# Attention and mLSTM outputs: the 64-row products grouped by bank, and the mLSTM's output gate emptied by VectorE before its sigmoids

## The chip, the cores and the metric

One core of a Trainium2 chip runs the kernel. The metric is device time in microseconds (us) from start to end, median of three runs. TensorE (PE in the profile) multiplies, VectorE (DVE), ScalarE (ACT) and GpSimd (POOL) work element by element, and SyncE (SP) issues most transfers. A matmul contracts over the rows (partitions) of its operands: up to 128 of them, here 128 or 64. It writes to a bank of PSUM, up to 512 f32 values in every partition here; the kernel has four banks (`mm`) for the large products and four (`ax`) for the small ones.

## The reference, cut to what matters

One decoder layer over 512 tokens and 1024 channels, in f32. Its mixer runs three branches on the same normalised input. Two of them carry a matrix state for each of four heads, with keys of 64 and values of 128 channels:

```python
# gated linear attention, chunk by chunk
o_inter = einsum('bhld,bhdv->bhlv', qi * exp(cum), state)
o = o_inter + einsum('bhij,bhjv->bhiv', scores, vi)

# mLSTM, chunk by chunk
scores = einsum('bhtd,bhsd->bhts', qi, ki) * exp(d_intra - m_t[..., None])
num = w_inter[..., None] * einsum('bhtd,bhdv->bhtv', qi, mem) + einsum('bhts,bhsv->bhtv', scores, vi)
den = w_inter * einsum('bhtd,bhd->bht', qi, norm) + scores.sum(-1)
h = num / maximum(abs(den), exp(-m_t))[..., None]
y_ml = sigmoid(mo) * h          # mo: a projection of the layer's input
```

The third branch is a state-space layer (S5) with a gelu. The branches are projected, weighted by sigmoid gates, summed and projected by `w_out`; a SwiGLU network of two large products follows.

## The kernel before, in words

The kernel takes chunks of 128 tokens, four of them (`t` = 0 to 3). A head's state has 64 rows, one for each key channel, so two heads lie in one tile: head `h = 2p + hh` has the rows `64 hh` to `64 hh + 63` of pair `p`. The output of a chunk adds two products for each head: the scores with the values (`ST` with `gv` in attention, L1169; `Sc` with `mvp` in the mLSTM, L1459), which contract over the 128 tokens of the chunk, and the scaled queries with the state before the chunk (`qE` with `Sg`, L1173; `qw` with `mem`, L1462), which contract over 64 rows. Chunk 0 has no state before it, so only the first. Two `ax` banks take a chunk, one for each `hh`; a bank holds the heads of both pairs side by side. mLSTM columns are 129, the last one for the denominator.

Attention's banks are emptied by VectorE into `og` (L226, four operations a chunk); ScalarE squares them, VectorE makes the norm and multiplies by the gate `gr`, and PE transposes the result (L1196 in `to_fm`). The mLSTM's banks go through ScalarE (absolute value) and VectorE (reciprocal, then `ym`, which multiplies by the gate `mo`), and are transposed in the same function. In `scores(t)`, PE multiplies keys and queries over 64 rows (L1448) and VectorE multiplies by the decay `Wd`.

Between such steps the large projections run: `fill(n)` takes the next pieces of a list of jobs (`gv`, `su`, `gr`, merge gates, `mx`, `mo`, `mv`, `glu`, ...). Each weight block comes by a transfer of SP (L319), is split into a high part `hi` by ScalarE and a rest `lo` by VectorE (both f32r), and is multiplied in three passes of 512 columns (L422 to L424, and L454 to L456 where tokens are the output's rows). `mo` is such a job: four banks, one for each chunk, emptied by `ev_mo` (L645). The next job, `mv`, needs the same four banks.

The program gives an order, but the framework schedules the mixer again, engine by engine, from its own estimates; only the head of the kernel and everything from the output projection on keep a written order. So an edit in the mixer may also move instructions that it does not name. The S5 branch runs among the `mo` products: its state products (L1314 and L1315) read `U`, `M`, `Xs` and `CA`; `Xs` comes from VectorE's scan, rotations and products, and `M` from SP's loads of `kd_d` (L1269). `conv` are the mLSTM's four tiles of queries and keys, made of four VectorE steps each and a silu; `Y` is the gelu of the S5 output, `rho` an activation of its decay, `WT` the copied states. Different functions of ScalarE need different tables, loaded by ACT_TABLE_LOAD.

Of the kernel before, what the change touches and what calls it, by code (L numbers as in the profile page):

```python
# [8 lines left out]
AF = mybir.ActivationFunctionType  # L9
OP = mybir.AluOpType  # L10
# [166 lines left out]
def _body(tc, A, out):  # L177
    nc = tc.nc
    act, dve, pool, pe, sp = nc.scalar, nc.vector, nc.gpsimd, nc.tensor, nc.sync
    from contextlib import ExitStack  # L180
    with ExitStack() as ctx:
        _emit(tc, nc, ctx, ExitStack, A, out, act, dve, pool, pe, sp)


def _emit(tc, nc, ctx, ExitStack, A, out, act, dve, pool, pe, sp):
# [23 lines left out]
    def slot(name="s", dt=F32, tag="s"):  # L209
        return pools[tag].tile([128, 512], dt, tag=tag, name=name)  # L210
# [4 lines left out]
    def ax_bank(name="ax"):  # L215
        return axp.tile([128, 512], F32, tag="ax", name=name)


    def tt(e, o, a, b, op):
        e.tensor_tensor(out=o, in0=a, in1=b, op=op)  # L220
# [4 lines left out]
    def stt(o, a, s, b, op0, op1):  # L225
        dve.scalar_tensor_tensor(out=o, in0=a, scalar=s, in1=b, op0=op0, op1=op1)  # L226

    def af(o, i, f, **kw):
        act.activation(out=o, in_=i, func=f, **kw)  # L229

    def cp(o, i, e=dve):
        e.tensor_copy(out=o, in_=i)
# [6 lines left out]
    mm = pe.matmul  # L239
# [69 lines left out]
    class Stream:  # L309
        loaded = done = 0  # L310
        raw, hl = {}, {}
        start = None
# [178 lines left out]
    i = 0  # L491
# [21 lines left out]
    ST = {}  # L513
# [46 lines left out]
    w, h, u, r = (st[:, 4 * i:4 * i + 4] for i in range(4))  # L560
# [9 lines left out]
    for t in range(4):  # L570
        tk = slice(t * 128, (t + 1) * 128)
# [51 lines left out]
    gv, gr, mo = {}, {}, {}  # L623
    conv = {}
# [19 lines left out]

    def ev_mo(t, ps):  # L645
        mo[t] = slot("mo", tag="v")
        af(mo[t], ps, AF.Sigmoid)

    def ev_conv(f):
        def e(ps):  # L650
# [163 lines left out]
    for f in range(4):  # L814
        job(f"mx{f}", fm_job(A["wmx"], f, ev_conv(f)))
    job("mo", tm_job(A["wmo"], ev_mo))
    job("mv", tm_job(A["wmv"], ev_mv), lambda: "v" in ML)
    glu_idx = [add_item(A["wgl"][j // 2][:, (j % 2) * 512:(j % 2 + 1) * 512], w=512) for j in range(4)]
# [111 lines left out]
    for p in range(2):  # L930
        ps = ax_bank()
# [149 lines left out]
    qk, qE, ecum, kdT, Sg = {}, {}, {}, {}, {}  # L1081
# [39 lines left out]
    for p in range(2):  # L1121
        qk[p] = slot("qk")
        tt(dve, qk[p], qT[p], kT[p], OP.mult)
        for t in range(4):
            mm(dps[:, t * 4 + p * 2:t * 4 + p * 2 + 2], lhsT=qk[p][:, t * 128:(t + 1) * 128], rhs=C("heads"),
               start=True, stop=True)
    cp(dg, dps[:, 0:16])
    for p in range(2):
# [10 lines left out]
        ps = ax_bank()  # L1139
# [6 lines left out]
    for p in range(2):  # L1146
        Sg[p] = slot("Sg", tag="y")
        for t in range(3):
            ps = ax_bank()
            mm(ps[:, 0:256], lhsT=kdT[p][:, t * 128:(t + 1) * 128], rhs=gv[t][:, p * 256:(p + 1) * 256],  # L1150
               start=True, stop=True)
            for h in range(2):
                r = slice(64 * h, 64 * h + 64)
                o = Sg[p][r, t * 128:(t + 1) * 128]
# [7 lines left out]
    ssg, rg = st3[:, 16:32], st3[:, 32:48]  # L1162
    for t in range(4):
        ps = [ax_bank(), ax_bank()]
        for h in range(4):
            p, hh = h // 2, h % 2
            o = ps[hh][:, p * 128:(p + 1) * 128]
            a = (t % 2) * 2 + hh
            mm(o, lhsT=ST[p, t // 2][:, a * 128:(a + 1) * 128], rhs=gv[t][:, h * 128:(h + 1) * 128],  # L1169
               start=True, stop=(t == 0))  # L1170
            if t > 0:
                r = slice(64 * hh, 64 * hh + 64)
                mm(o, lhsT=qE[p][r, t * 128:(t + 1) * 128], rhs=Sg[p][r, (t - 1) * 128:t * 128],  # L1173
                   start=False, stop=True)
        og[t] = slot("og")
        for h in range(4):
            sl = slice(h * 128, (h + 1) * 128)
            stt(og[t][:, sl], gv[t][:, sl], dg[:, t * 4 + h:t * 4 + h + 1],
                ps[h % 2][:, (h // 2) * 128:(h // 2 + 1) * 128], OP.mult, OP.add)
            junk = slot("junk")  # L1180
            af(junk[:, 0:128], og[t][:, sl], AF.Square, accum_out=ssg[:, t * 4 + h:t * 4 + h + 1])
        fill(1)
# [162 lines left out]
    mvp = vp.tile([128, 4, 4, 129], F32, name="mvp")  # L1345
# [3 lines left out]
    def mslot(name="m"):  # L1349
        return mp.tile([128, 512], F32, tag="m", name=name)  # L1350
# [36 lines left out]
    ps = ax_bank()  # L1387
# [6 lines left out]
    wI, qw, kw, mem = {}, {}, {}, {}  # L1394
    for p in range(2):
        ps = ax_bank()
# [3 lines left out]
    Wd = {}  # L1400
# [11 lines left out]
    for p in range(2):  # L1412
        qw[p] = mslot("qw")
        stt(qw[p], conv[p], 0.125, wI[p], OP.mult, OP.mult)
        ps = ax_bank()
# [8 lines left out]
    for p in range(2):  # L1424
        mem[p] = mslot("mem")
        for t in range(3):
            ps = ax_bank()
            mm(ps[:, 0:258], lhsT=kw[p][:, t * 128:(t + 1) * 128],
               rhs=mvp[:, t, 2 * p:2 * p + 2].rearrange("p h v -> p (h v)"), start=True, stop=True)
            for h in range(2):  # L1430
                r = slice(64 * h, 64 * h + 64)
                o = mem[p][r, t * 129:(t + 1) * 129]
# [6 lines left out]
    ym, Sc = {}, {}  # L1439

    def scores(t):
        tk = slice(t * 128, (t + 1) * 128)
        Sc[t] = mslot("Sc")
        for hh in range(2):
            ps = ax_bank()
            r = slice(64 * hh, 64 * hh + 64)
            for p in range(2):
                mm(ps[:, p * 128:(p + 1) * 128], lhsT=conv[2 + p][r, tk], rhs=conv[p][r, tk], start=True, stop=True)  # L1448
            v = lambda a: a.rearrange("p (q h i) -> p q h i", q=2, h=2)[:, :, hh]
            stt(v(Sc[t]), ps[:, 0:256].rearrange("p (q i) -> p q i", q=2), 0.125, v(Wd[t]), OP.mult, OP.mult)  # L1450

    def heads_out(t):
        ym[t] = slot("ym")
        for hh in range(2):
            ps = ax_bank()
            for p in range(2):
                o = ps[:, p * 129:(p + 1) * 129]
                h = 2 * p + hh
                mm(o, lhsT=Sc[t][:, h * 128:(h + 1) * 128], rhs=mvp[:, t, h], start=True, stop=(t == 0))  # L1459
                if t > 0:  # L1460
                    r = slice(64 * hh, 64 * hh + 64)
                    mm(o, lhsT=qw[p][r, t * 128:(t + 1) * 128], rhs=mem[p][r, (t - 1) * 129:t * 129],  # L1462
                       start=False, stop=True)
            den = st3[:, 32 + 4 * (t % 2) + 2 * hh:34 + 4 * (t % 2) + 2 * hh]
            pv_ = ps[:, 0:258].rearrange("p (q v) -> p q v", q=2)
            ac = st3[:, 48 + 4 * (t % 2) + 2 * hh:50 + 4 * (t % 2) + 2 * hh]
            af(ac.unsqueeze(2), pv_[:, :, 128:129], AF.Abs)
            ev = em.rearrange("p (t q h) -> p t q h", q=2, h=2)[:, t, :, hh]
            tt(dve, den, ac, ev, OP.max)
            dve.reciprocal(out=den, in_=den)  # L1470
            for p in range(2):
                h = 2 * p + hh
                sl = slice(h * 128, (h + 1) * 128)
                stt(ym[t][:, sl], ps[:, p * 129:p * 129 + 128], den[:, p:p + 1], mo[t][:, sl], OP.mult, OP.mult)

    scores(0)
    for t in range(4):
        if t < 3:
            decay(t + 1)
            fill(1)  # L1480
            scores(t + 1)
        heads_out(t)
        fill(1)
# [255 lines left out]
```

## Time and profile before

| | |
|---|---|
| runs | 917.51, 920.76, 921.31 us; median 920.76 |
| profiled execution | 917.74 us, of which the span is 915.9 |
| PE busy | 896.3 us, 98% |
| DVE busy | 574.0 us, 63% |
| ACT busy | 332.7 us, 36%; 31 table loads of 1283 ns among them |
| PE's granted clock | 9 tenths or more in all but the first of 40 slices |
| transfers | 120.79 MB, mean 132 GB/s |

The view that carries most is the timeline of an engine: start, busy time, line, output and inputs, shape, how many in a row, and in brackets the idle time before and what ended it. On PE an f32 product is two passes, which the timeline counts as x2; the f32r products of 512 columns are one each. Matmuls are pipelined, so the next one starts before the time of the one before has run out: what a piece of work costs is seen in the distance between starts.

### The profile page before, as it was taken

What the parts mean: (1) busy time and instruction counts of PE and PEld (TensorE: products, weight loads), DVE (VectorE), ACT (ScalarE), POOL (GpSimd) and SP (SyncE); (2) the same over time, 40 slices, a digit from 0 to 9 for tenths busy, and PEclk for the clock granted to TensorE, in tenths of its full rate; (3) what the DMA queues carried; (4) which work ended last, traced back from release to release, by engine and by line L of the source; (5) the groups of instructions that cost most, each with busy time, mean ns of one, the idle gap of its engine ahead of it and who ended that gap; (6) DMA issues with size and microseconds to landing.
All of it is one profiled execution on the core that took longest, in us unless ns stands there. A gap on an engine that the chain in (4) does not pass through costs nothing.

```text
span 915.9 us, 11578 instructions
## 1 busy us (share of the span) xinstructions
PE 896.3 (98%) x4334; PEld 726.7 (79%) x4334; DVE 574.0 (63%) x1140; ACT 332.7 (36%) x513; POOL 24.9 (3%) x68
## 2 busy tenths in 40 slices
PE   8999999999989999999999989999999999999997
PEld 7668887778878878778888867888888888888885
DVE  6848999879879974965669487634444333322215
ACT  4339323431442481622334454422332223211113
POOL 1010000000000000000010000000000000000000
PEclk8999999999999999999999999999999999999999
DMA  9661431234542442434455543533333333322304
GB/s 363 247 192 47 127 116 58 68 122 120 158 141 103 120 115 92 137 106 161 155 183 203 188 163 116 177 121 132 116 114 123 118 105 114 115 92 93 115 1 137
DMA packets 52193, 120.79 MB, mean 132 GB/s; under 512 B 13797, under 2 KB 19429, under 8 KB 52137
## 3 DMA queue, kind: packets, MB, share of 16 engines
q1 hardware_dynamic: 49944, 115.92, 37.9%
q0 software_dynamic: 1040, 2.38, 1.1%
q10 hardware_dynamic: 1152, 1.75, 0.5%
q8 instruction: 34, 0.56, 0.2%
q14 instruction: 23, 0.18, 0.1%
HBM read 113.21 MB, written 6.82 MB: 131 GB/s over the span
## 4 chain that ended last, share of the span: by engine, by line
PE 80%; DVE 15%; issue 2%; ACT 2%; DMA 1%; SPq 0%; DVEq 0%; ACTq 0%
PE mm L422 16%; PE mm L424 16%; PE mm L423 16%; PE y L1519 5%; PE y L1520 5%; PE y L1521 5%; DVE lo L220 2%; PE mm L455 2%; PE mm L454 2%; PE mm L456 2%; DVE ST L1108 1%; DVE Qp L220 1%; DVE D L220 1%; PE ax L1314 1%; PE ax L1315 1%
## 5 line engine op out<-in xcount | busy, mean ns | idle before, releaser
L229 ACT ACTIVATE hi<-raw 128x1024 fp32r<-128x1024 f32 (+2 forms) x157 | 151.9, 971 | 389.4 <-PE mm L423 161.4
L220 DVE TENSOR_TENSOR lo<-raw,hi 128x1024 fp32r<-128x1024 f32 (+2 forms) x157 | 174.6, 1114 | 152.3 <-ACT hi L229 151.6
L424 PE MATMUL mm<-h2hi,lo 128*128 128x512 f32 x320 | 124.6, 389 | 0.0
L423 PE MATMUL mm<-h2lo,hi 128*128 128x512 f32 x320 | 124.6, 389 | 0.0
L422 PE MATMUL mm<-h2hi,hi 128*128 128x512 f32 x320 | 124.5, 389 | 0.0
L424 PE MATMUL mm<-hT,lo 128*128 128x512 f32 x280 | 110.9, 396 | 3.1 <-DVE lo L220 3.1
L422 PE MATMUL mm<-hT,hi 128*128 128x512 f32 x280 | 112.3, 401 | 1.2 <-ACT hT L229 1.2
L423 PE MATMUL mm<-hT,hi 128*128 128x512 f32 x280 | 110.9, 396 | 0.5 <-DVE hT L226 0.4
L423 PEld LDWEIGHTS mm<-h2lo,hi 128*128 128x128 f32 x320 | 60.1, 188 | 12.6
L422 PEld LDWEIGHTS mm<-h2hi,hi 128*128 128x128 f32 x320 | 60.1, 188 | 12.5
L424 PEld LDWEIGHTS mm<-h2hi,lo 128*128 128x128 f32 x320 | 60.1, 188 | 12.3
L1521 PE MATMUL y<-hi,g 128*128 128x512 f32 x176 | 68.5, 389 | 0.0
L1520 PE MATMUL y<-lo,g 128*128 128x512 f32 x176 | 68.5, 389 | 0.0
L1519 PE MATMUL y<-hi,g 128*128 128x512 f32 x176 | 68.3, 389 | 0.0
L422 PEld LDWEIGHTS mm<-hT,hi 128*128 128x128 f32 x280 | 53.0, 189 | 16.8 <-issue 4.4
L220 DVE TENSOR_TENSOR sg<-sg,mm 128x512 f32<-128x512 f32 x36 | 24.7, 685 | 65.8 <-PE mm L424 65.8
L424 PEld LDWEIGHTS mm<-hT,lo 128*128 128x128 f32 x280 | 53.1, 190 | 14.9 <-DVE lo L220 3.5
L423 PEld LDWEIGHTS mm<-hT,hi 128*128 128x128 f32 x280 | 53.1, 190 | 11.9 <-DVE hT L226 1.3
L226 DVE SCALAR_TENSOR_TENSOR gacc<-raw,cact,gacc 128x512 f32<-128x512 f32 x56 | 41.9, 748 | 21.7 <-DMA raw<-ada 21.1
L455 PE MATMUL mm<-lo,hT 128*128 128x512 f32 x128 | 50.5, 395 | 0.4 <-DVE lo L220 0.4
L454 PE MATMUL mm<-hi,hT 128*128 128x512 f32 x128 | 49.8, 399 | 0.0
L456 PE MATMUL mm<-hi,hT 128*128 128x512 f32 x128 | 49.7, 391 | 0.0
(310 smaller groups left out, 1404.4 us busy)
## 6 DMA issues: line engine op xcount, KB each, us to landing
raw<-ada SPq DMA_DIRECT2D x48, 512.0 KB, 3.6
raw<-ffn SPq DMA_DIRECT2D x44, 512.0 KB, 3.4
raw<-wzg SPq DMA_DIRECT2D x24, 512.0 KB, 3.3
raw<-ffo SPq DMA_DIRECT2D x22, 512.0 KB, 3.3
raw<-wpr SPq DMA_DIRECT2D x24, 256.0 KB, 2.7
raw<-wout SPq DMA_DIRECT2D x8, 512.0 KB, 3.3
raw<-sweep SPq DMA_DIRECT2D x8, 384.0 KB, 9.0
xT<-xT SPq DMA_DIRECT2D x4, 512.0 KB, 5.6
```

The costliest lines, as they stand in the source:

```text
L220: e.tensor_tensor(out=o, in0=a, in1=b, op=op)
L226: dve.scalar_tensor_tensor(out=o, in0=a, scalar=s, in1=b, op0=op0, op1=op1)
L229: act.activation(out=o, in_=i, func=f, **kw)
L422: mm(ps, lhsT=whi, rhs=xhi, start=first, stop=False)
L423: mm(ps, lhsT=whi, rhs=xlo, start=False, stop=False)
L424: mm(ps, lhsT=wlo, rhs=xhi, start=False, stop=last)
L454: mm(ps[t], lhsT=xh[:, tk], rhs=hi[:, sl], start=(k == 0), stop=False)
L455: mm(ps[t], lhsT=xh[:, tk], rhs=lo[:, sl], start=False, stop=False)
L456: mm(ps[t], lhsT=xl[:, tk], rhs=hi[:, sl], start=False, stop=(k == 7))
L1519: mm(ps, lhsT=xhi, rhs=whi[:, sl], start=first, stop=False)
L1520: mm(ps, lhsT=xhi, rhs=wlo[:, sl], start=False, stop=False)
L1521: mm(ps, lhsT=xlo, rhs=whi[:, sl], start=False, stop=last)
```

## The change

In attention's output and in the mLSTM's (`heads_out`) the loop over heads becomes two: first the four 64-row products of a chunk, then the four 128-row products on top of them. In `scores` all four products are issued ahead of VectorE's two steps, with both banks taken first. In `ev_mo` VectorE copies each bank out of PSUM, and after the fourth copy ScalarE does the four sigmoids in place.

```diff
     def ev_mo(t, ps):
         mo[t] = slot("mo", tag="v")
-        af(mo[t], ps, AF.Sigmoid)
+        cp(mo[t], ps)
+        if t == 3:
+            for u in range(4):
+                af(mo[u], mo[u], AF.Sigmoid)
...
         ps = [ax_bank(), ax_bank()]
+
+        for h in range(4 if t else 0):
+            p, hh = h // 2, h % 2
+            r = slice(64 * hh, 64 * hh + 64)
+            mm(ps[hh][:, p * 128:(p + 1) * 128], lhsT=qE[p][r, t * 128:(t + 1) * 128],
+               rhs=Sg[p][r, (t - 1) * 128:t * 128], start=(p == 0), stop=False)
         for h in range(4):
             p, hh = h // 2, h % 2
-            o = ps[hh][:, p * 128:(p + 1) * 128]
             a = (t % 2) * 2 + hh
-            mm(o, lhsT=ST[p, t // 2][:, a * 128:(a + 1) * 128], rhs=gv[t][:, h * 128:(h + 1) * 128],
-               start=True, stop=(t == 0))
-            if t > 0:
-                r = slice(64 * hh, 64 * hh + 64)
-                mm(o, lhsT=qE[p][r, t * 128:(t + 1) * 128], rhs=Sg[p][r, (t - 1) * 128:t * 128],
-                   start=False, stop=True)
+            mm(ps[hh][:, p * 128:(p + 1) * 128], lhsT=ST[p, t // 2][:, a * 128:(a + 1) * 128],
+               rhs=gv[t][:, h * 128:(h + 1) * 128], start=(t == 0 and p == 0), stop=(p == 1))
...
         Sc[t] = mslot("Sc")
+        ps = [ax_bank(), ax_bank()]
+        for p in range(2):
+            for hh in range(2):
+                r = slice(64 * hh, 64 * hh + 64)
+                mm(ps[hh][:, p * 128:(p + 1) * 128], lhsT=conv[2 + p][r, tk], rhs=conv[p][r, tk], start=True, stop=True)
         for hh in range(2):
-            ps = ax_bank()
-            r = slice(64 * hh, 64 * hh + 64)
-            for p in range(2):
-                mm(ps[:, p * 128:(p + 1) * 128], lhsT=conv[2 + p][r, tk], rhs=conv[p][r, tk], start=True, stop=True)
...
         ym[t] = slot("ym")
+        pss = [ax_bank(), ax_bank()]
+        for h in range(4 if t else 0):
+            p, hh = h // 2, h % 2
+            r = slice(64 * hh, 64 * hh + 64)
+            mm(pss[hh][:, p * 129:(p + 1) * 129], lhsT=qw[p][r, t * 128:(t + 1) * 128],
+               rhs=mem[p][r, (t - 1) * 129:t * 129], start=(p == 0), stop=False)
+        for h in range(4):
+            p, hh = h // 2, h % 2
+            mm(pss[hh][:, p * 129:(p + 1) * 129], lhsT=Sc[t][:, h * 128:(h + 1) * 128], rhs=mvp[:, t, h],
+               start=(t == 0 and p == 0), stop=(p == 1))
         for hh in range(2):
-            ps = ax_bank()
-            for p in range(2):
-                o = ps[:, p * 129:(p + 1) * 129]
-                h = 2 * p + hh
-                mm(o, lhsT=Sc[t][:, h * 128:(h + 1) * 128], rhs=mvp[:, t, h], start=True, stop=(t == 0))
-                if t > 0:
-                    r = slice(64 * hh, 64 * hh + 64)
-                    mm(o, lhsT=qw[p][r, t * 128:(t + 1) * 128], rhs=mem[p][r, (t - 1) * 129:t * 129],
-                       start=False, stop=True)
+            ps = pss[hh]
```

The scheduler decides where these instructions come to stand. On PE, attention's chunk 1 before (`ax_1587` and `ax_1588` are its two banks, for the row halves A, rows 0 to 63, and B, 64 to 127; the numbers are those of buffers):

```order
L1169 MATMUL ax_1587<-gv_959,ST_118 128x128
L1173 MATMUL ax_1587<-Sg_1481,qE_1429 128x128
L1169 MATMUL ax_1587<-gv_959,ST_122 128x128
L1173 MATMUL ax_1587<-Sg_1512,qE_1443 128x128
L1169 MATMUL ax_1588<-gv_959,ST_118 128x128
L1173 MATMUL ax_1588<-Sg_1481,qE_1429 128x128
L1169 MATMUL ax_1588<-gv_959,ST_122 128x128
L1173 MATMUL ax_1588<-Sg_1512,qE_1443 128x128
```

After:

```order
L1172 MATMUL ax_1587<-Sg_1481,qE_1429 128x128
L1172 MATMUL ax_1587<-Sg_1512,qE_1443 128x128
L1177 MATMUL ax_1587<-gv_959,ST_118 128x128
L1177 MATMUL ax_1587<-gv_959,ST_122 128x128
L1172 MATMUL ax_1588<-Sg_1481,qE_1429 128x128
L1172 MATMUL ax_1588<-Sg_1512,qE_1443 128x128
L1177 MATMUL ax_1588<-gv_959,ST_118 128x128
L1177 MATMUL ax_1588<-gv_959,ST_122 128x128
```

The banks stay apart, and in each the two 64-row products stand before the two 128-row products. The mLSTM's chunk 1 has the same form.

On PE, the mLSTM's chunk 2 before (banks `ax_3683` and `ax_3693`; chunk 3 follows at once in the same form):

```order
L1459 MATMUL ax_3683<-mvp_3097,Sc_3601 128x129
L1462 MATMUL ax_3683<-mem_3439,qw_3402 128x129
L1459 MATMUL ax_3683<-mvp_3097,Sc_3601 128x129
L1462 MATMUL ax_3683<-mem_3473,qw_3410 128x129
L1459 MATMUL ax_3693<-mvp_3097,Sc_3601 128x129
L1462 MATMUL ax_3693<-mem_3439,qw_3402 128x129
L1459 MATMUL ax_3693<-mvp_3097,Sc_3601 128x129
L1462 MATMUL ax_3693<-mem_3473,qw_3410 128x129
```

After (banks `ax_3687` and `ax_3688`):

```order
L1463 MATMUL ax_3687<-mem_3443,qw_3406 128x129
L1463 MATMUL ax_3687<-mem_3477,qw_3414 128x129
L1463 MATMUL ax_3688<-mem_3443,qw_3406 128x129
L1463 MATMUL ax_3688<-mem_3477,qw_3414 128x129
L1467 MATMUL ax_3687<-mvp_3097,Sc_3605 128x129
L1467 MATMUL ax_3688<-mvp_3097,Sc_3605 128x129
L1467 MATMUL ax_3687<-mvp_3097,Sc_3605 128x129
L1467 MATMUL ax_3688<-mvp_3097,Sc_3605 128x129
```

Four 64-row products, the half A twice and the half B twice, then four 128-row products. Chunk 3 follows at once in the same form; so do attention's chunks 2 (A, A, B, B) and 3 (A, B, A, B), each by itself.

On ACT, a piece of the difference at the place where the `mo` products begin (`hi_2956` is the high part of the second weight block of `mo`; `Y_2849` and `rho_2943` belong to the S5 branch):

```order
-L229 ACTIVATE hi_2956<-raw_2799 128x1024
 L229 ACTIVATE WT_2773<-ax_2774 128x512
 L229 ACTIVATE WT_2773<-ax_2780 128x512
 L229 ACT_TABLE_LOAD
+L229 ACTIVATE conv_2826<-conv_2826 128x512
+L229 ACT_TABLE_LOAD
 L229 ACTIVATE Y_2849<-ax_2832 128x512
 L229 ACTIVATE rho_2943<-w5_732 128x256 x2
 L229 ACT_TABLE_LOAD
-L229 ACTIVATE conv_2826<-conv_2826 128x512
 L229 ACTIVATE conv_2883<-conv_2883 128x512
+L229 ACTIVATE hi_2956<-raw_2799 128x1024
```

One silu of `conv` with a table load of its own has moved ahead of the gelu, and `hi_2956` from ahead of `WT` to behind the second silu. Further on the four sigmoids of `mo` stand in a row where they were two pairs, with the two exponentials `wI` ahead of them. On DVE the four copies of `mo` stand ahead of `Wd` of chunk 0. On SP one load of the weights of `mv` has moved behind eight loads of `M`.

## Rows read from the trace of the kernel before

**Rows 1.** Page, busy us (share of the span) and instructions of an engine.

```profile
PE 896.3 (98%) x4334; PEld 726.7 (79%) x4334; DVE 574.0 (63%) x1140; ACT 332.7 (36%) x513; POOL 24.9 (3%) x68
```

**Rows 2.** Waits of PE, 175 to 425 us: total, times, longest.

```profile
PE mm L424 <- DVE lo L220: 3.1, 1, 3.1
PE ax L1196 <- DVE og L226: 0.7, 1, 0.7
```

**Rows 3.** Timeline of PE, 151 us: start, busy time, line, out<-in, shape, count.

```profile
151.11 0.61 PE L1169 MATMUL ax<-gv,ST 128*128 128x128 f32 x4
...
151.79 0.39 PE L424 MATMUL mm<-hT,lo 128*128 128x512 f32 x1
```

**Rows 4.** Timeline of PE, 369 to 376 us: 64-row products of the scores.

```profile
369.14 0.40 PE L424 MATMUL mm<-hi,lo 128*128 128x512 f32 x1
369.47 0.72 PE L1448 MATMUL ax<-conv 64*128 64x128 f32 x8
...
370.46 0.40 PE L422 MATMUL mm<-yhi,hi 128*128 128x512 f32 x1
...
373.88 0.39 PE L422 MATMUL mm<-hT,hi 128*128 128x512 f32 x1
374.20 0.71 PE L1448 MATMUL ax<-conv 64*128 64x128 f32 x4
...
375.18 0.39 PE L424 MATMUL mm<-hT,lo 128*128 128x512 f32 x1
```

**Rows 5.** Timeline of PE, attention's chunk 2.

```profile
158.54 0.39 PE L424 MATMUL mm<-hT,lo 128*128 128x512 f32 x1
158.77 0.38 PE L1169 MATMUL ax<-gv,ST 128*128 128x128 f32 x2
159.08 0.48 PE L1173 MATMUL ax<-Sg,qE 64*128 64x128 f32 x2
...
162.34 0.39 PE L423 MATMUL mm<-hT,hi 128*128 128x512 f32 x1
```

**Rows 6.** Timeline of DVE, attention's outputs of chunks 2 and 3.

```profile
163.43 1.11 DVE L226 SCALAR_TENSOR_TENSOR og<-gv,st,ax 128x128 f32<-128x128 f32 x4
167.36 0.61 DVE L226 SCALAR_TENSOR_TENSOR og<-gv,st,ax 128x128 f32<-128x128 f32 x2 [2.81 <-PE ax L1173]
168.19 0.60 DVE L226 SCALAR_TENSOR_TENSOR og<-gv,st,ax 128x128 f32<-128x128 f32 x2 [0.23 <-PE ax L1173]
```

**Rows 7.** Timeline of PE at three places.

```profile
314.32 0.33 PE L1315 MATMUL ax<-Xs,CA 128*128 128x64 f32 x2
...
333.51 0.48 PE L454 MATMUL mm<-hi,hT 128*128 128x512 f32 x1
...
411.83 1.25 PE L1196 MATMUL ax<-ident,ym 128*128 128x128 f32 x10
```

**Rows 8.** Timeline of DVE at three places.

```profile
311.45 1.71 DVE L220 TENSOR_TENSOR Xs<-x,y 64x252 f32<-64x252 f32 x4
...
337.88 1.23 DVE L220 TENSOR_TENSOR lo<-raw,hi 128x1024 fp32r<-128x1024 f32 x1 [1.54 <-ACT hi L229]
...
407.64 1.13 DVE L226 SCALAR_TENSOR_TENSOR ym<-ax,st,mo 128x128 f32<-128x128 f32 x4
```

**Rows 9.** Timeline of ACT, 294 to 331 us.

```profile
294.67 1.06 ACT L229 ACTIVATE hi<-raw 128x1024 fp32r<-128x1024 f32 x1 [5.17 <-PE mm L423]
...
297.60 1.28 ACT L229 ACT_TABLE_LOAD   x1
...
303.22 1.29 ACT L229 ACTIVATE conv<-conv 128x512 f32<-128x512 f32 x2 [0.92 <-DVE conv L226]
...
330.50 1.08 ACT L229 ACTIVATE mo<-mm 128x512 f32<-128x512 f32 x2
```

**Rows 10.** Costliest groups: copies of mv (busy us, mean ns, idle before).

```profile
L232 DVE COPY mvp<-mm 128x512 f32<-128x512 f32 x4 | 2.7, 692 | 2.0 <-PE mm L456 2.0
```

**Rows 11.** SP's queue, loads of M.

```profile
306.14 3.62 SPq L1269 DMA_DIRECT2D M<-kd_d  x8
```

More of the change, by code (lines that the diff above doesn't have):

```diff
@@ L1443, in scores @@
         Sc[t] = mslot("Sc")
+        ps = [ax_bank(), ax_bank()]
[3 more added lines that the diff above has]
+                mm(ps[hh][:, p * 128:(p + 1) * 128], lhsT=conv[2 + p][r, tk], rhs=conv[p][r, tk], start=True, stop=True)
         for hh in range(2):
-            ps = ax_bank()
-            r = slice(64 * hh, 64 * hh + 64)
-            for p in range(2):
-                mm(ps[:, p * 128:(p + 1) * 128], lhsT=conv[2 + p][r, tk], rhs=conv[p][r, tk], start=True, stop=True)
             v = lambda a: a.rearrange("p (q h i) -> p q h i", q=2, h=2)[:, :, hh]
-            stt(v(Sc[t]), ps[:, 0:256].rearrange("p (q i) -> p q i", q=2), 0.125, v(Wd[t]), OP.mult, OP.mult)
+            stt(v(Sc[t]), ps[hh][:, 0:256].rearrange("p (q i) -> p q i", q=2), 0.125, v(Wd[t]), OP.mult, OP.mult)
     def heads_out(t):
         ym[t] = slot("ym")
-        for hh in range(2):
-            ps = ax_bank()
-            for p in range(2):
-                o = ps[:, p * 129:(p + 1) * 129]
-                h = 2 * p + hh
-                mm(o, lhsT=Sc[t][:, h * 128:(h + 1) * 128], rhs=mvp[:, t, h], start=True, stop=(t == 0))
-                if t > 0:
-                    r = slice(64 * hh, 64 * hh + 64)
-                    mm(o, lhsT=qw[p][r, t * 128:(t + 1) * 128], rhs=mem[p][r, (t - 1) * 129:t * 129],
-                       start=False, stop=True)
+        pss = [ax_bank(), ax_bank()]
[8 more added lines that the diff above has]
+               start=(t == 0 and p == 0), stop=(p == 1))
+        for hh in range(2):
+            ps = pss[hh]
             den = st3[:, 32 + 4 * (t % 2) + 2 * hh:34 + 4 * (t % 2) + 2 * hh]
```

## The prediction

> **What bounds the kernel.** I read the busy table first: TensorE (PE) is busy 98% of the span [rows 1]. Then PE's waits from the attention outputs (175 us) to the end of the mLSTM (425): two rows, 3.1 and 0.7 us [rows 2]. So a microsecond taken out of PE's own row of work reaches the end, unless another engine has to come earlier too; each saving below is followed to where PE next waits. The profiled execution took 917.74 us around a span of 915.9; the sum is made against 917.74. The median shown, 920.76, is 3.02 us (0.33%) above it, and the result is scaled by 920.76/917.74. Half a per cent, about what a measurement of this kernel can tell from no change, is 4.6 us.
>
> **Price of a switch between 128-row and 64-row products.** Each f32 product stands as two passes (x2 in the rows), and 512-column matmuls start 0.23 us apart. A block is charged from the start that the next matmul would have had without it to the start of the second matmul behind it, less one spacing. Four 128-row passes between 512-column matmuls: 151.11 to 151.79 less 0.23, 0.45 us, or 0.115 a pass with no switch [rows 3]. Four 64-row passes of one row half: 373.88 to 375.18 less two spacings, 0.85; less 4 x 0.115 that leaves 0.39 for two switches, 0.19 each [rows 4]. One attention chunk with its alternating products: 158.54 to 162.34 less two spacings, 3.34 for 16 passes and 8 switches; less 16 x 0.115 = 1.84 that is 1.50, again 0.19 each [rows 5]. And eight 64-row passes of both row halves, in the order A, A, B, B: 369.14 to 370.46 less two spacings, 0.87 [rows 4]. That is no more than four passes of one half took: the two halves run side by side, and four passes (0.46) cost nothing.
>
> A rule of the Trainium skill speaks against this last step. "TensorE: Matmul & The Clock Gate", Part 3, under "What overlaps and what doesn't", holds that matmuls start and end strictly in program order; in the order A, A, B, B only the seam of the halves would then overlap, and the gain from it would be near zero. The trace does not agree (0.87 against 0.85 us for twice the passes), so I keep the trace's price and give the other a chance as a rival.
>
> **The PE terms.** The changed order keeps the places of the chunks and changes their insides. Chunk 0 of both mixers has no 64-row product. In chunk 1 of both, the two banks stay apart, each with its two 64-row products and then its two 128-row ones: 8 switches become 4, nothing side by side, 4 x 0.19 = 0.75 us. In chunks 2 and 3 all four 64-row products stand together, then the four 128-row ones: 0.87 + 8 x 0.115 = 1.79 in place of 3.34, 1.55 us each. Attention: 0.75 + 2 x 1.55 = 3.9. The mLSTM has the same counts: 3.9. Together 48 switches become 16 and 4 x 0.46 us run beside other passes: 7.8. The scores edit changes nothing on PE: pairs and places are as before.
>
> **Attention: what passes on.** VectorE (DVE) empties these banks (og). It works without a pause to 164.54, then idles 2.81 us for the last products of chunk 3, does two, idles 0.23, does two, and ends at 168.79 [rows 6]. With PE 3.9 earlier the banks are full at about 164.2 and DVE runs all four from 164.54 (four in a row took 1.11): it ends at 165.65, 3.1 earlier. Behind that its timeline shows no pause from 171 to 197, and in that stretch stands og times the gate, for which PE's transposes (L1196) wait 0.7 us [rows 2]. So PE has 3.9 and DVE 3.1: PE's wait grows by 0.8, and 3.1 goes on. The wait of 3.1 (L424) later ends a chain of ScalarE (ACT) and DVE that moves along with both.
>
> "TensorEngine Tiling (Array Packing)" of the Trainium skill, Performance Considerations, warns that packing speeds up TensorE and not the emptying of PSUM, which may become the bottleneck. The trace bears this out for 0.8 of the 3.9 us; were it wholly so, the first rival would follow.
>
> **mLSTM: what passes on.** The last ym is done at 407.64 + 1.13 = 408.77, and PE's transposes first read it at 411.83: 3.06 us of slack [rows 7, 8]. DVE pauses here for PE's products, through ACT. It needs about 3.3 us for the ym of chunks 2 and 3 from 402.6 on, so ym is ready near 406, for a use that moves to about 408. All 3.9 passes; the few waits of PE behind 425 follow its own output products and move along. Gross gain: 3.1 + 3.9 = 7.0 us.
>
> **The gate mo.** Before, four ACT sigmoids read PSUM in two pairs (1.08 the pair) with table loads around them [rows 9]; after, four DVE copies like mvp's (0.69 each, 2.7 together) [rows 10] empty the banks and the sigmoids run in one go. ACT saves two loads of 1.28 here and gets one back near 298; it is not the bound, and mo is read only near 380, so PE gains nothing. The cost is 2.7 us of DVE ahead of Wd and qw. DVE's pauses there hold part of it (1.54 at 337.88 [rows 8]). The banks must be free for mv's first product at 333.51 [rows 7], and the first copy can be done near 332. I take 0, bounds 0 and 1.5.
>
> **What the new order does at 295 to 316.** Here I expect a loss. The silu of the first conv tile, with a table load of its own, now stands ahead of the gelu Y, and hi of the gate's second weight block (hi_2956, 1.06 at 294.67) stands behind both and behind the next silu. Laid end to end on ACT from 297.60 with [rows 9]: load 1.28, wait for DVE's last tap to about 299.8 (its taps now stand ahead of those of the third tile), silu 0.65, load 1.28, gelu and two rho (as many columns as two silus) 1.3, load 1.28, silu 0.65, hi 1.06: done near 306.1 instead of 295.7. DVE's lo behind it then waits some 2.7 us and ends at 307.3; PE reads it 25 products of 0.23 ahead of L1315, near 308.6. With the rest of DVE's queue (taps, scan, rotations, another lo, Xs: some 8 us in the timeline) the last Xs is done at about 315.4 in place of 311.45 + 1.71 = 313.16, and PE's L1315 reads Xs from 314.32 [rows 7, 8]. A slack of 1.16 turns into a wait of about 1.1. Bounds: 0 (pauses of DVE take it up) and 2.7 (the whole stall of lo). I take 1.1. SP also puts one load of mv's weights behind the eight M loads, which end at 306.14 + 3.62 = 309.8 [rows 11], some 8 us later; PE needs it only for mv's products, at 333.51 and after, so nothing.
>
> **Sum.** 3.1 + 3.9 - 1.1 = 5.9 us: 911.8 on the profiled run's scale, 914.8 on the median's.
>
> **Rivals.**
> - **DVE keeps the attention gain.** If og and what follows it (squares on ACT, statistics on DVE) do not come earlier, PE waits 0.7 + 3.9 at L1196 and only mLSTM's part is left: 3.9 - 1.1 = 2.8, so 914.9, or 917.9 on the median's scale, no change. For: DVE is full from 171 to 197. Against: its idle 2.81 ends with PE alone [rows 6].
> - **The halves do not run side by side,** so the change does only half of what it says. Then 16 switches go in each mixer, 3.0 us each: 3.0 + 3.0 - 1.1 = 4.9, so 912.8, or 915.9: on the border of faster. For: in chunk 3 of attention the halves alternate (A, B, A, B), an order that no row shows. Against: the block of eight at 369.47 [rows 4]. The rule in the skill named above would give this.
> - **The other side: ACT's new order holds DVE and PE at 300 to 335.** If the first silu starts only at 303.2, where it stood [rows 9], everything behind it on ACT is 3.4 us later, and with it lo and Xs: PE waits 1.1 + 3.4 = 4.5 at L1315. If DVE's copies of mo (2.7) then come too late for mv's banks, and the four sigmoids in a row (2.2) delay Wd and what follows it, the waits add up to 9.4: 917.74 - 7.0 + 9.4 = 920.1, or 923.2. It turns the sign from 7.0 us of waits on. For: the slack at L1315 is 1.16. Against: DVE does the taps of this tile earlier in the new order, and one wait pays for the next, since a PE that has waited needs everything later.
>
> **How the numbers follow.** Forecast 0.64, DVE keeps it 0.14, no side by side 0.14, the other side 0.08. The forecast's own range is 912.5 to 917 (waits of 0 to 2.7, medians that scatter by 1 to 2 us). Range over the cases: low 910.5 (no new wait and a quick median), high 919, which takes in the first two rivals and leaves out most of the last. Faster by over 0.5% (under 916.2): 0.58 of the forecast, 0.07 of the second rival, 0.01 of the first, 0.66. Slower: the last rival, 0.08. Same: the rest, 0.26.
>
> **What would show it.** After: chunks 2 and 3 of 1.8 us in both mixers, with the 64-row block of eight near 0.87 in either order of the halves; DVE's four og of chunk 3 in one row; PE's wait at the og transposes near 1.5; a wait at L1315 of 0 to 2.7; none at mv's first product. A 64-row block of 1.3 us shows the second rival, a wait over 3 at the og transposes the first, waits above 7 us between 295 and 335 the third. Waits of PE at another place would make the prediction wrong without any of them.

## The result, and the profile after

The changed kernel takes 911.14 us (median of 4 runs, 909.74 to 912.69) against 920.81 for the kernel before: ratio 0.9905, 95% interval 0.9888 to 0.9921. Timed a second time it took 912.39 us, ratio 0.9918 (0.9903 to 0.9933). So it is faster by 0.7 to 1.1% over the two intervals. One of the five executions of experiment 9 took 2270.16 us and stays out of that experiment's ratio. The profiled execution took 910.4 us around a span of 908.6, 7.3 us less than the span before.

The busy table, as in [rows 1], says that PE is still the bound and has lost 7.6 us of its 896.3:

```profile
PE 888.7 (98%) x4334; PEld 723.1 (80%) x4334; DVE 575.7 (63%) x1144; ACT 331.0 (36%) x512; POOL 24.9 (3%) x68
```

PE's waits from 175 to 425 us, as in [rows 2] (on the left the line that waits, on the right the one it waits for, then total, times and longest): the wait for attention's transposes (now L1200) is 1.6 us where it was 0.7, the other one is unchanged, and there is no third.

```profile
PE mm L424 <- DVE lo L220: 3.1, 1, 3.1
PE ax L1200 <- DVE og L226: 1.6, 1, 1.6
```

Attention's chunk 2 in PE's timeline, to set beside [rows 5] (before 158.54 to 162.34):

```profile
158.03 0.40 PE L424 MATMUL mm<-hT,lo 128*128 128x512 f32 x1
158.35 0.72 PE L1172 MATMUL ax<-Sg,qE 64*128 64x128 f32 x8
159.01 1.16 PE L1177 MATMUL ax<-gv,ST 128*128 128x128 f32 x8
159.92 0.48 PE L422 MATMUL mm<-hT,hi 128*128 128x512 f32 x1
160.24 0.39 PE L423 MATMUL mm<-hT,hi 128*128 128x512 f32 x1
```

158.03 to 160.24 less two spacings of 0.23 is 1.75 us, where the forecast had 1.79 and the kernel before 3.34. The eight 64-row passes take 0.66 from start to start; in chunk 3, in the order A, B, A, B, 0.65 (162.84 to 163.49). So the halves run side by side in either order.

DVE behind it, to set beside [rows 6]: eight og in one go without a pause, done at 165.86, and the multiplications by the gate from 184.95.

```profile
163.71 2.15 DVE L226 SCALAR_TENSOR_TENSOR og<-gv,st,ax 128x128 f32<-128x128 f32 x8
166.86 0.46 DVE L223 TENSOR_SCALAR st<-st 128x16 f32<-128x16 f32 x3 [1.00 <-ACT junk L229]
...
184.95 4.28 DVE L226 SCALAR_TENSOR_TENSOR og<-og,st,gr 128x128 f32<-128x128 f32 x16
```

And chunk 1 of the mLSTM on PE, where the profile shows something that the forecast did not have. The first block of this chunk's 64-row products (L1463, half A) stands directly behind the second scores block (L1452, half B), and their passes start 0.01 to 0.02 us apart:

```profile
382.39 0.39 PE L423 MATMUL mm<-ylo,hi 128*128 128x512 f32 x1
382.70 0.37 PE L1452 MATMUL ax<-conv 64*128 64x128 f32 x1
382.72 0.37 PE L1463 MATMUL ax<-mem,qw 64*128 64x129 f32 x1
...
383.14 0.27 PE L1452 MATMUL ax<-conv 64*128 64x128 f32 x1
383.15 0.27 PE L1463 MATMUL ax<-mem,qw 64*128 64x129 f32 x1
383.36 0.71 PE L1467 MATMUL ax<-mvp,Sc 128*128 128x129 f32 x4
383.82 0.47 PE L424 MATMUL mm<-yhi,lo 128*128 128x512 f32 x1
384.14 0.39 PE L422 MATMUL mm<-hT,hi 128*128 128x512 f32 x1
```

Before, the scores block went into 128-row products, and 64-row ones came later:

```profile
385.09 0.39 PE L423 MATMUL mm<-ylo,hi 128*128 128x512 f32 x1
385.41 0.71 PE L1448 MATMUL ax<-conv 64*128 64x128 f32 x4
386.05 0.49 PE L1459 MATMUL ax<-mvp,Sc 128*128 128x129 f32 x2
386.47 0.49 PE L1462 MATMUL ax<-mem,qw 64*128 64x129 f32 x2
...
388.06 0.39 PE L422 MATMUL mm<-hT,hi 128*128 128x512 f32 x1
```

Now eight passes of two kinds share one block of 0.66 us and its two switches. Between the same two 512-column matmuls the whole piece takes 1.75 us (382.39 to 384.14) instead of 2.97: 1.22 less, which is four switches of 0.19 and four passes of 0.115 side by side. The forecast had two switches, 0.38, for it.

**Where the time went.** One number per place says most: how much earlier PE starts the same matmul than in the profile of before, which I call its lead (us, worked out from the two timelines; the numbers in the heads are the matmul's start in the profile of before).

| kernel | ahead of attention's outputs (153.83) | behind its chunk 3 (168.08) | og transposes (188.16) | at 269.51 | ahead of the mLSTM's outputs (355.96) | behind chunk 1 (390.08) | behind chunk 3 (406.93) | end |
|---|---|---|---|---|---|---|---|---|
| changed | -0.27 | 3.68 | 2.81 | 2.51 | 2.66 | 4.28 | 7.47 | 7.32 |
| mLSTM alone | 1.12 | 1.12 | 1.14 | -1.44 | -1.53 | 0.04 | 3.23 | 3.35 |
| attention alone | 1.76 | 5.71 | 4.85 | 2.78 | 3.17 | 3.18 | 3.18 | 3.21 |
| gate alone | 1.65 | 1.65 | 1.66 | -0.53 | -0.59 | -0.55 | -0.55 | -0.51 |
| both groupings | 2.59 | 6.54 | 5.68 | 3.17 | 3.54 | 5.13 | 8.32 | 8.35 |
| ... 128-row first | 0.06 | 4.02 | 3.16 | 3.04 | 3.42 | 4.21 | 7.39 | 6.64 |
| ... one row half | 0.06 | 3.14 | 2.69 | 0.56 | 0.92 | 2.51 | 4.84 | 4.80 |
| changed, again | 1.13 | 5.08 | 4.20 | 1.73 | 2.09 | 3.71 | 6.90 | 6.90 |

Differences along a row are what counts. The first column is how the execution began: it scatters by 3 us between single executions, before any changed instruction. Attention gives 3.95 to its last product, of which 3.08 pass the transposes (2.81 + 0.27). The mLSTM's outputs give 1.62 in chunk 1 and 3.19 in chunks 2 and 3, together 4.81. The sum, 7.9 us, lies in the interval of the ratio (7.3 to 10.3 us).

### The profile page after: what moved, and what is told of

It reads as the page before. It is cut to its first block, busy times and chain, and to the rows that moved or that the text cites. A ratio compares the mean times of both kernels' runs of the same rounds, so it can differ in the third digit from the quotient of the medians.

```text
span 908.6 us, 11582 instructions
## 1 busy us (share of the span) xinstructions
PE 888.7 (98%) x4334; PEld 723.1 (80%) x4334; DVE 575.7 (63%) x1144; ACT 331.0 (36%) x512; POOL 24.9 (3%) x68
## 3 DMA queue, kind: packets, MB, share of 16 engines
q10 hardware_dynamic: 1152, 1.75, 0.5%
## 4 chain that ended last, share of the span: by engine, by line
PE 77%; DVE 17%; issue 2%; ACT 2%; DMA 1%; SPq 0%; DVEq 0%; ACTq 0%
PE mm L422 16%; PE mm L423 16%; PE mm L424 16%; PE y L1527 5%; PE y L1526 5%; PE y L1528 5%; DVE lo L220 3%; PE mm L455 2%; PE mm L454 2%; PE mm L456 2%; DVE ST L1111 1%; DVE Qp L220 1%; DVE o L220 1%; DVE D L220 1%; PE ax L1318 1%
```

## The experiments

**1. The mLSTM alone.** Edit: the parts of the diff in `scores` and `heads_out`, nothing else. Its order differs from before only on PE.

```diff
         ym[t] = slot("ym")
+        pss = [ax_bank(), ax_bank()]
+        for h in range(4 if t else 0):
...
+        for h in range(4):
```

> The mLSTM grouping alone (with the scores edit), attention and the gate mo as before. Its order differs from before on PE alone. Theory: 4.9 us faster than before (ratio near 0.9947): chunks 2 and 3 give 3.1, chunk 1 gives 1.7, because its first 64-row block now stands beside the second scores block of 64 rows and runs next to it. Rival: chunk 1 gives 0.75 as counted ahead of the result and the rest of the 4.9 comes from elsewhere; then 3.9 (0.9958). In the profile: PE's lead over the kernel before steps up by 1.7 and 3.1 us at these chunks under the theory, by 0.75 and 3.1 under the rival.

Measured: 914.99 us, ratio 0.9948 (0.9932 to 0.9965). In the table 1.57 in chunk 1 and 3.19 behind it, 4.76 in all: the theory's figures, not 0.75 and 3.1; the ratio alone could not tell the two apart. The loss of 2.6 between 188.16 and 269.51, where nothing was changed, is the clock (last section).

**2. Attention alone.** Edit: the part of the diff at L1164 to L1174.

```diff
         ps = [ax_bank(), ax_bank()]
+        for h in range(4 if t else 0):
...
         for h in range(4):
```

> Attention's grouping alone. Theory: PE comes 4.0 us earlier at the end of chunk 3, DVE 3.1, PE's wait at the og transposes grows from 0.74 to about 1.6, and 3.1 us reach the end (ratio near 0.9966). Rival (DVE keeps it): the wait grows to over 3 and less than 1 us is left.

Measured: 914.91 us, ratio 0.9953 (0.9938 to 0.9968). 3.95 at the last product, 3.09 behind the transposes, where the wait is 1.6 us. DVE kept 0.9 of 3.95, as expected. The new order at 295 to 316 comes with this edit: neither this run nor the changed kernel shows a PE wait there.

**3. The gate alone.**

```diff
-        af(mo[t], ps, AF.Sigmoid)
+        cp(mo[t], ps)
+        if t == 3:
+            for u in range(4):
+                af(mo[u], mo[u], AF.Sigmoid)
```

> The gate mo alone: four DVE copies, then four sigmoids in one go; all products in the order of before. Theory: no change within 1 us (ratio 0.999 to 1.001), since ACT is not waited for and the copies fit before mv's products. Rival: it is a part of the gain (the runs of the changed kernel gained 8.7 us by their ratio where the one profile shows 7.3): 1.4 us faster (0.9985).

Measured: 919.58 us, ratio 1.0004 (0.9992 to 1.0015). The theory holds: nothing. PE's lead is -0.53 at 269.51 and -0.55 at 390.08 and 406.93. In between, at 333 us, three transposes of `conv` have come to stand earlier, against the expectation; the 0.3 us that this moves is back by 356.

**4. Both groupings, the gate as before.**

```diff
         mo[t] = slot("mo", tag="v")
-        cp(mo[t], ps)
-        if t == 3:
-            for u in range(4):
-                af(mo[u], mo[u], AF.Sigmoid)
+        af(mo[t], ps, AF.Sigmoid)
```

> Both groupings without the gate's edit. Theory: the whole gain of the changed kernel, 7 to 9 us (ratio 0.990 to 0.992). Rival: without the copies the gain falls short by 1.4 us or more, because ACT's sigmoids hold mo's banks until mv wants them.

Measured: 910.11 us, ratio 0.9899 (0.9884 to 0.9914). The theory holds: all of the gain is here, 3.09 and 4.78 in the table.

**5. The 128-row products first.** Edit in `heads_out` of experiment 4: the two loops change places, so that the scores block meets a 128-row product again.

```diff
+        for h in range(4):
+            p, hh = h // 2, h % 2
+            mm(pss[hh][:, p * 129:(p + 1) * 129], lhsT=Sc[t][:, h * 128:(h + 1) * 128], rhs=mvp[:, t, h],
+               start=(p == 0), stop=(t == 0 and p == 1))
         for h in range(4 if t else 0):
...
-               rhs=mem[p][r, (t - 1) * 129:t * 129], start=(p == 0), stop=False)
-        for h in range(4):
...
+               rhs=mem[p][r, (t - 1) * 129:t * 129], start=False, stop=(p == 1))
```

> Both groupings without the gate's edit, but in the mLSTM the 128-row products stand first and the four 64-row products behind them; everything else in the same places. The number of switches inside the chunks stays. Theory (the seam): chunk 1 loses what it had from standing beside the scores' 64-row block, two switches and four passes side by side, 0.84 us; PE's lead over the kernel before then grows by 0.75 us in chunk 1 and by 3.1 in chunks 2 and 3; 0.8 us slower than with the 64-row products first. Rival: the larger gain in chunk 1 comes from the grouping itself, and nothing changes.

Measured: 911.83 us, ratio 0.9912 (0.9898 to 0.9927); beside experiment 4 the times alone would be inconclusive, but the table is not: chunk 1 gives 0.79 in place of 1.59, chunks 2 and 3 still 3.18. PE's timeline at chunk 1 shows the scores by themselves:

```profile
381.97 0.71 PE L1449 MATMUL ax<-conv 64*128 64x128 f32 x4
382.61 0.71 PE L1459 MATMUL ax<-mvp,Sc 128*128 128x129 f32 x4
383.25 0.71 PE L1464 MATMUL ax<-mem,qw 64*128 64x129 f32 x4
383.89 0.50 PE L424 MATMUL mm<-yhi,lo 128*128 128x512 f32 x1
```

Three blocks of 0.64 where the changed kernel has two (0.66 and 0.46). The seam with the scores is what chunk 1 gained beyond the forecast.

**6. One row half for all.** Edit in experiment 4: the 64-row products read rows 0 to 63 for both halves.

```diff
-            r = slice(64 * hh, 64 * hh + 64)
+            r = slice(0, 64)
```

> Both groupings without the gate's edit; order and places of all instructions are the same, but the 64-row products of attention's and the mLSTM's outputs all read row half 0 to 63 of queries and state (the heads of the other half use the wrong rows). So nothing can run beside another row half. Theory: each of the four contiguous chunks is 4 x 0.115 = 0.46 us longer and the block of eight takes 1.31 instead of 0.87; with chunk 1 of the mLSTM (0.23 to 0.46, beside the scores' second half), PE is 2.1 to 2.3 us later by 425 us, and by 0.9 less where attention's wait swallows its part. Rival (in strict program order only the seam overlaps): almost nothing changes, under 0.5 us.

Measured: 911.93 us, ratio 0.9910 (0.9895 to 0.9925). Attention's chunk 2 on PE:

```profile
157.69 0.40 PE L424 MATMUL mm<-hT,lo 128*128 128x512 f32 x1
158.02 1.16 PE L1169 MATMUL ax<-Sg,qE 64*128 64x128 f32 x8
159.10 1.16 PE L1174 MATMUL ax<-gv,ST 128*128 128x128 f32 x8
160.02 0.48 PE L422 MATMUL mm<-hT,hi 128*128 128x512 f32 x1
```

The same eight passes take 1.08 us from start to start instead of 0.66. They still go to two banks, so what lets them run side by side is the other row half, not the other bank. In the table attention gives 3.08 at its last product (3.95 with two halves) and 2.63 behind the transposes, the mLSTM 3.92 instead of 4.78: 1.3 us in all at the end, 1.73 on PE itself, about 0.43 for each of the four chunks. The rival (under 0.5 us) falls; the theory's 2.1 to 2.3 was too much mainly by the seam, which this edit does not touch (the block beside the scores' half B is half A either way, and chunk 1 gives 1.59 in both).

**7 and 8. Part of attention's scaling on ScalarE,** to get back what DVE kept. Edit in experiment 4, for chunks 0 and 1, then for all four:

```diff
-            stt(og[t][:, sl], og[t][:, sl], rg[:, t * 4 + h:t * 4 + h + 1], gr[t][:, sl], OP.mult, OP.mult)
+            af(og[t][:, sl], og[t][:, sl], AF.Copy, scale=rg[:, t * 4 + h:t * 4 + h + 1])
...
+        tt(dve, og[t], og[t], gr[t], OP.mult)
```

> Both groupings without the gate's edit; ScalarE scales attention's chunks 0 and 1 by the norm (8 operations), VectorE only multiplies them by the gate (2 operations of 512 columns), chunks 2 and 3 as before. Theory: the 16 VectorE operations of 0.27 us pace the 16 transposes, which take 4.3 us there; with half of them on ScalarE the wait of 1.6 us and part of the pacing go, 1.5 to 3 us faster than both groupings alone, 10.5 to 12 us faster than before (0.987 to 0.989). Rival: VectorE is full there, and what is taken off the wait comes back as a wait some microseconds later; no gain over both groupings.

> As the one with ScalarE on chunks 0 and 1, but with all four chunks scaled by ScalarE (16 operations, some 0.22 us apart, 3.5 us). Theory: ScalarE now paces the transposes; the gain is smaller than with two chunks, 0 to 1.5 us over both groupings alone. Rival: VectorE's free time counts more than ScalarE's pace, and it is as fast or faster than with two chunks.

Measured: 914.45 us, ratio 0.9939 (0.9927 to 0.9951), and 914.11, 0.9932 (0.9915 to 0.9949). Both theories fall: they are slower than the groupings alone. Both rivals came: no gain, and four chunks about as fast as two. PE's waits with two chunks on ScalarE:

```profile
PE ax L1202 <- DVE og L220: 4.1, 1, 4.1
PE mm L424 <- DVE lo L220: 2.3, 3, 1.5
PE ax L1256 <- DVE bs L232: 1.1, 1, 1.1
```

The transposes (L1202) stand at the same place among PE's matmuls as in experiment 4, and DVE starts the multiplications by the gate when it did in the changed kernel (184.92 and 184.95). But it does the eight of chunks 2 and 3 first, and PE's first four transposes wait for a product that stands behind them:

```profile
184.92 2.18 DVE L226 SCALAR_TENSOR_TENSOR og<-og,st,gr 128x128 f32<-128x128 f32 x8
187.02 0.69 DVE L220 TENSOR_TENSOR og<-og,gr 128x512 f32<-128x512 f32 x1
187.76 1.11 PE L1202 MATMUL ax<-ident,og 128*128 128x128 f32 x4 [4.06 <-DVE og L220]
```

So the wait grew from 1.6 to 4.1. With all four chunks on ScalarE it is 2.6 us in two pieces, and both runs have a wait for `lo` near 222 to 225 us (1.5 and 2.0) that experiment 4 does not have. Another order of DVE's operations was not tried. What these two leave open is whether the 0.9 us can be had back.

**9. The scores behind the outputs.** Edit in experiment 4:

```diff
             decay(t + 1)
             fill(1)
-            scores(t + 1)
         heads_out(t)
+        if t < 3:
+            scores(t + 1)
         fill(1)
```

> Both groupings without the gate's edit, and in the mLSTM the scores of chunk t+1 are issued behind the outputs of chunk t. In the order the 64-row blocks now stand in 16 changes between 64 and 128 rows instead of 20, and chunk 1 has its four 64-row products together, three of the four scores as well. Theory: 4 x 0.19 and some 0.46 more side by side, 1.2 us faster than both groupings alone, 9 to 10.5 us faster than before (0.9885 to 0.990). Rival: the later scores make VectorE and PE wait at the next chunk's products, and the gain is lost.

Measured: 909.19 us, ratio 0.988 (0.9864 to 0.9896). Between 362 and 408 us the trace has 16 changes between 64 and 128 rows where experiment 4 has 20. From 355.96 to the end PE's lead grows by 6.2 us where experiment 4 has 4.8: 1.4 more for an expected 1.2, and no new wait. The times alone do not separate it from experiment 4; the intervals overlap.

**10. One 64-row block for outputs and scores.** Edit: those of experiments 5 and 9 together.

> As the one with the scores behind, and in each mLSTM chunk the 128-row products stand first, so that its 64-row products and the scores of the next chunk make one block. 11 or 12 changes between 64 and 128 rows in the order. Theory: 8 x 0.19 = 1.5 and some 0.9 us side by side, 2.4 us faster than both groupings alone, 10 to 12 us faster than before (0.987 to 0.989). Rival: the 128-row products now need the scores' product with the decay at once, PE waits for VectorE there, and it is no faster than both groupings.

Measured: 907.56 us, ratio 0.9868 (0.985 to 0.9886): faster than before and than the changed kernel (ratios of the latter 0.9905 and 0.9918). In the profile, chunk 1 of the mLSTM (L1464) and the scores of chunk 2 (L1449):

```profile
382.84 0.40 PE L424 MATMUL mm<-yhi,lo 128*128 128x512 f32 x1
383.08 1.05 PE L1459 MATMUL ax<-mvp,Sc 128*128 128x129 f32 x8
384.06 0.72 PE L1464 MATMUL ax<-mem,qw 64*128 64x129 f32 x8
384.61 0.61 PE L1449 MATMUL ax<-conv 64*128 64x128 f32 x4
385.14 0.50 PE L422 MATMUL mm<-hT,hi 128*128 128x512 f32 x1
```

All eight 64-row passes of the outputs and four of the eight of the next scores stand between two switches; the other four still stand by themselves, at 389.67. Behind chunk 2 all sixteen make one block. The trace has 12 changes instead of 20. From 355.96 to the end the lead grows by 7.3 us (0.72 to 8.01), 2.5 more than in experiment 4, for an expected 2.4; PE shows no new wait.

**11. The changed kernel beside them.**

> The changed kernel itself, timed beside the others of this call. Theory: the gate's edit does nothing, so it lies with both groupings alone: ratio to before 0.9895 to 0.9915. Rival: the gate's edit costs or gives more than 1.5 us on top of the groupings, outside that range.

Measured: 912.39 us, ratio 0.9918 (0.9903 to 0.9933): just above the expected range, but not apart from experiment 4 by the intervals, and 4.81 for the mLSTM, 3.07 behind the transposes in the table.

## Why the prediction was right, and where it was not

The time came out faster, as forecast, and within the wide range (910.5 to 919), but 3.7 us below the figure given (911.14 against 914.8), and below the range that the forecast gave for itself (912.5 to 917). Two terms were wrong, both the same way, by 0.9 and 1.1 us; with them the sum of 5.9 becomes the 7.9 that PE's own times show.

- **Price of a switch and of a pass side by side:** right. Contiguous chunks 1.75 us for a forecast 1.79. Experiment 6 shows by itself what running side by side is worth: 0.43 us a chunk (forecast 0.46). The rule of program order in "TensorE: Matmul & The Clock Gate" of the Trainium skill, Part 3, "What overlaps and what doesn't", does not hold for these products: in the order A, A, B, B eight passes take 0.66 us, and 1.08 with one half alone.
- **Attention:** right. 3.95 on PE (3.9), 3.08 passed on (3.1), wait at the transposes 1.64 (near 1.5). DVE ran all og of chunk 3 in one go.
- **mLSTM:** the size was off, 4.8 for 3.9. The step that failed is "the same counts": the forecast counted the switches inside the outputs and left out the neighbour. In chunk 1 the block in front is made of 64 rows too, so two more switches and four passes go (0.84 by the forecast's own prices; 0.80 by experiments 4 and 5).
- **The gate:** right, nothing.
- **The loss at 295 to 316:** wrong, 0 for 1.1. The stall itself came nearly as worked out: DVE's lo waits 2.58 us for ACT (2.7), and the last Xs is done at 312.42. That is 3.0 us ahead of the forecast's 315.4, of which PE's lead at this place makes 2.6:

```profile
303.41 1.22 DVE L220 TENSOR_TENSOR lo<-raw,hi 128x1024 fp32r<-128x1024 f32 x1 [2.58 <-ACT hi L229]
...
310.70 1.72 DVE L220 TENSOR_TENSOR Xs<-x,y 64x252 f32<-64x252 f32 x4
```

  PE starts its first product with Xs at 312.38, without a wait (0.04 us before the last of the four Xs is done, so it reads an earlier one):

```profile
312.15 0.39 PE L455 MATMUL mm<-lo,hT 128*128 128x512 f32 x1
312.38 0.33 PE L1319 MATMUL ax<-Xs,CA 128*128 128x64 f32 x2
```

  That product is 1.94 us ahead of the one in [rows 7], not 2.6: the new order has put three more matmuls of 0.23 us in front of it, and they filled the time. With the 0.4 us that DVE came earlier than forecast, the 1.1 are gone. The forecast moved DVE by the new order and left PE's place as it was. The table has no loss here: 2.51 at 269.51, 2.66 at 355.96.
- **Rivals:** DVE did keep some of attention's gain, but only 0.9 us, where the forecast had 0.8; the halves do run side by side; the other side did not come (no wait of PE between 295 and 335 us).
- **The rest of the 3.7 us:** open. By PE's own times the change is worth 7.9 us; the ratio of the runs says 8.7 and the two medians lie 9.7 apart. The interval, 7.3 to 10.3 us, has all three, and no profile shows where more than 7.9 would come from.

## What to carry to other kernels

Where products of half the rows alternate with full ones, count the changes of height along PE's whole order, over the seams to the neighbours, and put all half-row work of both halves into one block: here, for f32 products of 128 columns, 0.19 us for each change avoided and 0.11 for each pass that runs beside one of the other half. A gain on PE has to be followed to the next place where PE waits; what another engine can't give earlier is kept there, 0.9 of 3.95 us in attention. When a new order delays one engine, look at what the same order puts in front of the waiting instruction on the other.

## What the runs showed of the hardware that was not expected

**The clock after a wait.** PE's granted clock falls to about half (1.2 of 2.4 GHz) at the end of its wait of 3.1 us in some executions and not in others: in eight of the eleven profiles here that have this wait, not in those of before, of the changed kernel as it was first profiled and of experiment 5. The stretches around it with the mLSTM alone (columns: window, its length, busy time and instructions of PE, of PEld, of DVE, ACT and POOL, then PE's granted clock, DMA share, GB/s):

```profile
191.00:194.00 3.00, 3.00 (x10) 2.29 (x10) 3.00 (x6) 1.74 (x4) 0.00 (x0) 0.63 0.43 114
254.00:258.30 4.30, 1.23 (x6) 0.73 (x5) 4.20 (x8) 0.00 (x0) 0.00 (x0) 0.97 0.00 0
258.30:261.00 2.70, 2.70 (x7) 2.12 (x8) 2.59 (x7) 0.00 (x0) 0.00 (x0) 0.50 0.57 194
```

and in the profile of the kernel before, for PE alone:

```profile
191.00:194.00 3.00, 3.00 (x13) 1.00 0.12 25
254.00:258.30 4.30, 1.23 (x7) 1.00 0.00 0
258.30:261.00 2.70, 2.70 (x12) 1.00 0.57 194
```

Seven matmuls in 2.7 us against twelve, behind the same wait. It costs 1.6 us there, and 1.0 near 192 us, behind the wait of the transposes (PE's lead in this run: 1.14 at 188.16, 0.13 at 257, -1.44 at 269.51). Near the transposes the clock falls in all of the thirteen profiles but those of before and of experiment 5 (0.72 to 0.86 from 183 to 195 us, against 1.00). So the sum of the forecast was made against an execution without either fall.

How much of the scatter between executions this makes is not shown. The 37 executions of the kernel before that stood beside the experiments have spans of 915.7 to 919.9 us, and lower mean clocks go with longer ones, but loosely: 918.6 to 919.3 at 0.987, 917.5 to 919.9 at 0.989, 915.8 to 916.7 at 0.99, 916.5 to 917.5 at 0.991. The mean also counts the first 26 us, where the clock is lower too (0.80 in the profile of before). Why it falls in one execution and not in the next stays open.
